# First layer of a hybrid decoder trunk: norm sums by TensorE, first chunk scaled from PSUM, k and q finished bank by bank

## The chip, the cores and the metric

The kernel runs on one core of one Trainium2 chip. The metric is device time in microseconds (us) of one launch, lower is better. All inputs lie in HBM when it starts and the result is written back to HBM.

## The reference

Two layers, each a token-mixing sub-layer and a SwiGLU sub-layer, on 512 tokens of width 1024 in float32. The change touches only the beginning of the first layer: the modulation, the norm of x, the first part of the input projection (k and q of the DeltaNet mixer) and what waits for it.

```python
c_act = jax.nn.silu(c)
for layer in range(DEPTH):
    mod = jnp.einsum('bd,de->be', c_act, w_mod[layer]) + b_mod[layer]
    shift1, scale1, gate1, shift2, scale2, gate2 = [m[:, None, :] for m in jnp.split(mod, 6, axis=-1)]
    h = rms_norm(x, mix_norm_w[layer]) * (1.0 + scale1) + shift1
    proj = jnp.einsum('btd,de->bte', h, w_in[layer])
    dn_qkv, dn_z, dn_a, dn_b, gm_uv, sw_qkv = jnp.split(proj, IN_SPLITS, axis=-1)
    y_a = deltanet_mixer(dn_qkv, dn_z, dn_a, dn_b, ...)   # causal conv of 4 taps and silu on q, k, v first
    ...
    x = x + gate1 * jnp.einsum('bte,ed->btd', y, w_out[layer])
    ...
```

`rms_norm` is `x * rsqrt(mean(x*x) + 1e-6) * w`, with the mean over the 1024 features.

## The kernel before, in words

x lies transposed in SBUF: 8 chunks `xs[0..7]` of 128 features by 512 tokens. The products are made in a three-pass form: both operands are split into a rounded part `hi` and a rest `lo` (type fp32r), and `mm3` issues hi·hi, hi·lo and lo·hi, each 128 rows by 128 columns of weights against 512 tokens. Splitting a weight piece takes one ACT instruction (`hi`) and one DVE instruction (`lo`).

Weights stream in as pieces of 512 KB: SP issues one DMA per piece into a ring of `N_RAW = 4` raw buffers, and a buffer comes free when its piece has been used. Weight pieces are split into a ring of `N_RING = 3` hi/lo pairs; a pair comes free when the matmuls that read it are done. In the first layer the pieces come in threes: two of the modulation matrix (`("mod", 0, c)` and `("mod", 0, 8 + c)`), then `("t", 0, c)`, which holds row chunk c of the weights of all 8 tiles of k and q. A modulation piece is consumed by one DVE instruction, a multiply with the broadcast condition and a sum along the row, that leaves one column of shift or scale.

`first()` does the start of the first layer, in coroutines that a planner interleaves:

- `squares()` takes each chunk of x as it lands: ACT squares it, DVE adds it to a running sum `a`, and `warm` issues a 128x256 matmul on it whose result nobody reads.
- `scale()` calls `inv_rms`: four matmuls of `a` with a column of ones give the sum over the features (128 tokens each, one output column each), DVE computes the reciprocal root (`rsqrt`, 9 small instructions), four matmuls with the identity broadcast it over the partitions into a bank, and ACT copies it into the SBUF slot `rs`.
- `chunk(c)` waits for `rs` and for the two modulation columns of c; ACT makes the gain `gg`, DVE multiplies x by gain and `rs` (`xn`), ACT adds the shift and rounds (`h[c].hi`), DVE makes the rest (`h[c].lo`).
- The main part then takes all 8 PSUM banks, one per tile of k and q, and runs chunk after chunk over all of them: 8 `mm3`, 24 matmuls, a chunk. All banks are complete only after the last chunk.

Then `layer` starts a `conv_of` on each of the 8 banks: ACT copies the bank to SBUF, which frees it, ACT scales the copy by the last tap, DVE adds three taps, ACT applies silu. The next projection, `ab`, needs four free banks.

What sets the order: there is no fixed list. `Plan` builds the program by running the coroutines against its own estimate of every instruction's duration, always taking the ready one with the lowest priority number, and each engine then executes its instructions in the order in which they were emitted. A change of a few instructions can therefore move others. The instructions are all recorded by one helper, so the profile gives L235 as the line of everything, and groups are told apart by the tiles' names: `w` a work slot, `xs` a chunk of x, `raw` a landed weight piece, `hi`/`lo` its split, `mod` the modulation columns, `s` a small tile, `cst` the constants (ones and identity among them), `b` a PSUM bank. A float32 matmul shows as two records on PE, an fp32r one as one.

Two places in `loader` and `splitter` matter below. The constants are loaded behind x:

```python
for c in range(KC):
    Q.dma_start(out=xs[c], in_=xT[:, c, :])
Q.dma_start(out=cst[:, 0:C_TRIU], in_=consts[:, 0:C_TRIU])
```

and a piece is split when the ring has room:

```python
if not raws[0] or (len(arena.free) < loose if loose else hold[0] or used[0] >= N_RING):
    return None
```

Of the kernel before, what the change touches and what calls it, by code (L numbers as in the profile page):

```python
# [88 lines left out]
class Plan:  # L89
# [106 lines left out]
    def spawn(self, gen, prio, name):  # L196
        t = Task(gen, prio, name)
        self.tasks.append(t)
        return t
# [84 lines left out]
def _trunk(ctx, tc, xT, cb, consts, prm, gmp, wmod, wt, wn, wab, wo, wo2, wf1, wf2, out):  # L284
# [29 lines left out]
    def bank(n=1, spare=0):  # L314

        yield banks.need(n + spare)
        got = [banks.get() for _ in range(n)]
        return got[0] if n == 1 else got
# [22 lines left out]
    def hs(h):  # L341
        return slice(h * P, (h + 1) * P)
# [175 lines left out]
    def wcols(w, j, n=128, pitch=None):  # L518
        if isinstance(w[0], list):
            return wcols((w[0][j * n // T], w[1][j * n // T]), j % (T // n), n)  # L520
        a = j * (pitch or n)
        return w[0][:, a:a + n], w[1][:, a:a + n]

    def mod_done(l, es):
        return tuple(mod_ok[l, e] for e in es)
# [28 lines left out]
    def mm3(ps, w, x, first, last):  # L554

        PE.matmul(ps, w[0], x[0], start=first, stop=False)
        PE.matmul(ps, w[0], x[1], start=False, stop=False)
        PE.matmul(ps, w[1], x[0], start=False, stop=last)
# [36 lines left out]
    def inv_rms(a, b0, n, warm=None):  # L595

        yield a[:, b0 * P:(b0 + n) * P]
        ps = yield from bank()
        for b in range(n):
            PE.matmul(ps[:, b:b + 1], a[:, hs(b0 + b)], ones[:, 0:1], start=True, stop=True)  # L600
        if warm:
            warm(a, 3)
        v = small(n)
        V.tensor_scalar(v, ps[:, 0:n], 1.0 / D, EPS, op0=ALU.mult, op1=ALU.add)
        bankf(ps)
        r = rsqrt(v, n)
        yield r
        rb = yield from bank()
        for b in range(n):
            PE.matmul(rb[:, hs(b0 + b)], r[:, b:b + 1].to_broadcast([P, P]), ident, start=True, stop=True)  # L610
        yield rb
        return rb
# [707 lines left out]

    def first():

        a = slot()

        bw = yield from bank()

        def warm(t, n=1):

            for _ in range(n):
                PE.matmul(bw[:, 0:256], t[:, 0:P], t[:, 0:256], start=True, stop=True)  # L1330

        def squares():
            yield x_ok
            for c in range(KC):
                yield S, xs[c]
                sq = slot() if c else a
                S.activation(sq, xs[c], AF.Square)
                yield V, sq
                warm(sq)
                if c:  # L1340
                    V.tensor_tensor(a, a, sq, op=ALU.add)
                    free(sq)

        sq = spawn(squares(), 0, "squares")
        rs = slot()

        def scale():
            yield sq
            rb = yield from inv_rms(a, 0, NB, warm)
            free(a)  # L1350
            S.activation(rs, rb, AF.Copy)
            bankf(rb)
            yield rs
            warm(rs, 3)
            bankf(bw)

        sc = spawn(scale(), 0, "scale")
        h = [Pair() for _ in range(KC)]

        def chunk(c):  # L1360
            yield sc, mod_done(0, (c, 8 + c))
            yield S, mods[0][:, c:c + 1], mods[0][:, 8 + c:9 + c]
            gg = small(1)
            nw = prs[0][:, L_NW + c:L_NW + c + 1]
            S.activation(gg, mods[0][:, 8 + c:9 + c], AF.Identity, scale=nw, bias=nw)
            yield V, gg
            xn = slot()
            V.scalar_tensor_tensor(xn, xs[c], gg, rs, op0=ALU.mult, op1=ALU.mult)
            yield S, xn
            h[c].hi, h[c].lo = slot(F32R), slot(F32R)  # L1370
            S.activation(h[c].hi, xn, AF.Identity, bias=mods[0][:, c:c + 1])
            yield V, h[c].hi
            V.scalar_tensor_tensor(h[c].lo, xn, mods[0][:, c:c + 1], h[c].hi[:].bitcast(F32), op0=ALU.add, op1=ALU.subtract)
            free(xn)
            h[c].ok[0].done = h[c].ok[1].done = True

        ts = [spawn(chunk(c), 0, f"h{c}") for c in range(KC)]
        yield sc
        pss = yield from bank(8)
        for c in range(KC):  # L1380
            w = yield from take("t", 0, c)
            x = yield from operand(h[c], FULL)
            for j in range(8):
                mm3(pss[j], wcols(w, j), x, c == 0, c == KC - 1)
                yield
            drop(w)
        yield tuple(ts)
        free(rs)
        return h, pss

    def layer(l, h, kq):

# [35 lines left out]
        def conv_of(i, ps):  # L1428
            return spawn(conv(ps, i, cw, AF.Silu if i < n_silu else AF.Tanh), rank()["conv" if i < 8 else "convv"], f"conv{i}")
# [94 lines left out]
        ts = spawn(gmlp(l, vg), rank()["gm"], "gmlp")  # L1524

        if l == 0:
            kT = [conv_of(i, ps) for i, ps in enumerate(kq[:4])]
            qT = [conv_of(4 + i, ps) for i, ps in enumerate(kq[4:])]

        def qss_of(qT):  # L1530
            r = yield from sumsq_heads(qT)
# [275 lines left out]
```

## Time and profile before

| | us |
|---|---|
| median of 3 runs | 1484.37 (1483.23 to 1485.97) |
| profiled execution, its own time | 1484.25 |
| span of its instructions | 1482.5 |
| TensorE (PE) busy | 1460.3 |
| DVE busy | 886.4 |
| ACT busy | 593.5 |
| mean granted clock of TensorE | 0.996 |

The span runs from the first to the last instruction; 1.75 us of the execution's own time lie around it. Busy time of an engine is the time covered by its records. The granted clock is given as a share of the full 2.4 GHz; 0.50 is 1.2 GHz. The clock column has no entry ahead of 13.83 us and shows 1.00 there, so that for the first 14 us the pace of the matmul records has to be read instead.

### The profile page before, as it was taken

Reading aid. Unit: us, or ns where it says so; the run is one execution under the profiler, and the core shown is the slowest. Engines: PE = TensorE matmul, PEld = TensorE weight load, DVE = VectorE, ACT = ScalarE, POOL = GpSimd, SP = SyncE. Lnnn points to the kernel's source line nnn. Section 1 sums busy time; section 2 is a strip of 40 time slices with the busy share of each in tenths; the row PEclk is TensorE's granted clock in tenths of the full one; section 3 lists DMA queues with packets and bytes.
Section 4 is the critical chain, followed back from the end, with each engine's and each line's share of the span. In section 5 each row is a group of like instructions: output and inputs, shape, how many; then the busy total and the mean of one; then the engine's idle time right before and its main releaser. Section 6 shows DMA issues by size and latency. Waiting matters only on the chain.

```text
span 1482.5 us, 19988 instructions
## 1 busy us (share of the span) xinstructions
PE 1460.3 (99%) x7810; PEld 1235.4 (83%) x7810; DVE 886.4 (60%) x1836; ACT 593.5 (40%) x1047; POOL 40.7 (3%) x60
## 2 busy tenths in 40 slices
PE   7999999999999999999999999999999999999998
PEld 5777998887988888888897889987789888888887
DVE  7788888946865555555476687656476333333332
ACT  4484426575432212222345533647544222222221
POOL 0001000000000000000000300100000000000000
PEclk9999999999999999999999999999999999999999
DMA  8723453503176665665322232121151332223331
GB/s 297 261 72 118 110 163 117 161 20 121 56 227 199 190 194 192 191 197 185 104 91 82 64 102 70 36 94 36 31 164 44 99 99 95 92 98 100 99 103 53
DMA packets 70638, 179.04 MB, mean 121 GB/s; under 512 B 25104, under 2 KB 25744, under 8 KB 70544
## 3 DMA queue, kind: packets, MB, share of 16 engines
q1 hardware_dynamic: 70544, 177.77, 37.5%
q8 instruction: 61, 1.00, 0.3%
q14 instruction: 33, 0.27, 0.1%
HBM read 174.53 MB, written 3.21 MB: 120 GB/s over the span
## 4 chain that ended last, share of the span: by engine, by line
PE 97%; DVE 1%; ACT 1%; DMA 0%; issue 0%; SPq 0%; ACTq 0%; DVEq 0%
PE b L235 97%; DVE w L235 1%; ACT w L235 1%; DMA xs<-in_xT_dram 0%; DVE s L235 0%; DVE raw L235 0%; DVE xs L235 0%; SPq L235 0%; DVE lo L235 0%; DVE mod L235 0%; ACT hi L235 0%; ACTq L235 0%; DVEq L235 0%
## 5 line engine op out<-in xcount | busy, mean ns | idle before, releaser
L235 PE MATMUL b<-w,hi 128*128 128x512 f32 (+1 forms) x2748 | 844.5, 389 | 2.5 <-ACT w L235 1.6
L235 PEld LDWEIGHTS b<-w,hi 128*128 128x128 f32 x2748 | 509.6, 188 | 110.8 <-issue 6.7
L235 PE MATMUL b<-w,lo 128*128 128x512 f32 (+1 forms) x1374 | 531.2, 387 | 0.0
L235 ACT ACTIVATE hi<-raw 128x1024 fp32r<-128x1024 f32 (+2 forms) x215 | 222.6, 1037 | 600.2 <-PE b L235 414.8
L235 DVE TENSOR_TENSOR lo<-raw,hi 128x1024 fp32r<-128x1024 f32 (+2 forms) x215 | 258.9, 1206 | 258.9 <-ACT hi L235 258.1
L235 PEld LDWEIGHTS b<-w,lo 128*128 128x128 f32 x1374 | 258.4, 188 | 52.3
L235 PE MATMUL b<-w,w 128*128 128x128 f32 (+2 forms) x1808 | 214.9, 284 | 4.0 <-ACT w L235 2.6
L235 PE MATMUL b<-hi,w 128*128 128x512 f32 (+2 forms) x768 | 214.8, 367 | 2.9 <-ACT w L235 2.9
L235 PEld LDWEIGHTS b<-w,w 128*128 128x128 f32 (+1 forms) x1808 | 199.2, 182 | 20.6 <-ACT w L235 10.2
L235 ACT ACTIVATE w<-b 128x512 f32<-128x512 f32 (+1 forms) x221 | 118.1, 560 | 137.0 <-PE b L235 126.0
L235 PEld LDWEIGHTS b<-hi,w 128*128 128x128 f32 x768 | 146.9, 213 | 24.1 <-issue 6.0
L235 PE MATMUL b<-lo,w 128*128 128x512 f32 (+2 forms) x384 | 137.7, 359 | 0.0
L235 DVE CUSTOM_DVE_ANT_0 raw<-raw,cact,pr 128x1024 f32<-128x1024 f32 x96 | 122.4, 1279 | 0.7 <-DMA raw<-in_wmod_dram 0.7
L235 DVE TENSOR_TENSOR w<-w,b 128x512 f32<-128x512 f32 x68 | 46.8, 688 | 125.5 <-PE b L235 124.7
L235 ACT ACTIVATE w<-w 128x512 f32<-128x512 f32 (+3 forms) x188 | 94.0, 519 | 22.9 <-DVE w L235 22.4
L235 PEld LDWEIGHTS b<-lo,w 128*128 128x128 f32 x384 | 81.4, 212 | 7.7
L235 DVE TENSOR_TENSOR w<-w,w 128x512 fp32r<-128x512 f32 (+2 forms) x104 | 68.1, 662 | 26.7 <-ACT w L235 26.1
L235 DVE SCALAR_TENSOR_TENSOR xs<-b,mod,xs 128x512 f32<-128x512 f32 (+1 forms) x56 | 37.1, 672 | 55.5 <-PE b L235 55.3
L235 PE MATMUL b<-cst,w 128*128 128x128 f32 (+1 forms) x416 | 57.5, 270 | 0.0
L235 PEld LDWEIGHTS b<-cst,w 128*128 128x128 f32 x416 | 49.4, 145 | 7.5 <-issue 1.0
L235 DVE SCALAR_TENSOR_TENSOR w<-w,cw,w 128x509 f32<-128x509 f32 (+2 forms) x72 | 51.8, 753 | 0.9 <-ACT w L235 0.2
L235 ACT ACTIVATE w<-w,mod 128x256 fp32r<-128x256 f32 (+1 forms) x56 | 29.8, 539 | 48.2 <-DVE w L235 48.2
(85 smaller groups left out, 652.4 us busy)
## 6 DMA issues: line engine op xcount, KB each, us to landing
raw<-in_wf_dram SPq DMA_DIRECT2D x132, 512.0 KB, 3.8
raw<-in_wmod_dram SPq DMA_DIRECT2D x96, 512.0 KB, 3.3
raw<-in_wt_dram SPq DMA_DIRECT2D x36, 512.0 KB, 3.5
raw<-in_wn_dram SPq DMA_DIRECT2D x36, 512.0 KB, 3.3
raw<-in_wo_dram SPq DMA_DIRECT2D x16, 320.0 KB, 2.9
raw<-in_wo_dram SPq DMA_DIRECT2D x6, 512.0 KB, 3.5
raw<-in_wab_dram SPq DMA_DIRECT2D x4, 544.0 KB, 5.7
xs<-in_xT_dram SPq DMA_DIRECT2D x8, 256.0 KB, 5.7
```

What stands on the lines that cost most here:

```text
L235: r = f(*args, **kw)
```

## The change

All of it is in `first()`, with one loop in `layer` that takes the banks as they come.

1. The running sum on DVE (7 additions of 128x512) goes. Instead, for every chunk, the four matmuls with a column of ones run on that chunk's square, and the eight chunks accumulate in one bank: 32 such matmuls in place of 4. The `warm` matmul stays, ahead of them; three `warm` behind the sums become two.
2. The broadcast reciprocal root is written over the same bank. Chunk 0 is multiplied from that bank instead of from the copy `rs`; the others wait for `rs` as before.
3. Chunks 0 to 5 run as before. Chunks 6 and 7 are taken together: for each bank, three matmuls of chunk 6 and three of chunk 7, after which the bank is handed to its `conv_of` at once.

```diff
@@ first() @@
-        a = slot()
...
-        def squares():
+        rs = slot()
+        got = Flag()
+
+        def scale():
+
             yield x_ok
+            ps = yield from bank()
+            sqs = [slot() for _ in range(KC)]
             for c in range(KC):
                 yield S, xs[c]
-                sq = slot() if c else a
-                S.activation(sq, xs[c], AF.Square)
-                yield V, sq
-                warm(sq)
-                if c:
-                    V.tensor_tensor(a, a, sq, op=ALU.add)
-                    free(sq)
-
-        sq = spawn(squares(), 0, "squares")
-        rs = slot()
-
-        def scale():
-            yield sq
-            rb = yield from inv_rms(a, 0, NB, warm)
-            free(a)
-            S.activation(rs, rb, AF.Copy)
-            bankf(rb)
+                S.activation(sqs[c], xs[c], AF.Square)
+                yield sqs[c]
+                warm(sqs[c])
+                for b in range(NB):
+                    PE.matmul(ps[:, b:b + 1], sqs[c][:, hs(b)], ones[:, 0:1], start=(c == 0 and b == 0), stop=(c == KC - 1),
+                              skip_group_check=True)
+            warm(sqs[KC - 1], 2)
+            v = small(NB)
+            V.tensor_scalar(v, ps[:, 0:NB], 1.0 / D, EPS, op0=ALU.mult, op1=ALU.add)
+            r = rsqrt(v, NB)
+            yield r
+            for b in range(NB):
+                PE.matmul(ps[:, hs(b)], r[:, b:b + 1].to_broadcast([P, P]), ident, start=True, stop=True)
+            got.value = ps
+            got.done = True
+            free(*sqs)
+            yield ps
+            S.activation(rs, ps, AF.Copy)
             yield rs
             warm(rs, 3)
             bankf(bw)
...
         def chunk(c):
-            yield sc, mod_done(0, (c, 8 + c))
+            yield got, mod_done(0, (c, 8 + c))
...
-            yield V, gg
+            rb = rs
+            if not c:
+                rb = got.value
+            else:
+                yield sc
+            yield V, gg, rb
             xn = slot()
-            V.scalar_tensor_tensor(xn, xs[c], gg, rs, op0=ALU.mult, op1=ALU.mult)
+            V.scalar_tensor_tensor(xn, xs[c], gg, rb, op0=ALU.mult, op1=ALU.mult)
+            if not c:
+                yield sc
+                bankf(rb)
...
-        for c in range(KC):
+        for c in range(KC - 2):
             w = yield from take("t", 0, c)
             x = yield from operand(h[c], FULL)
             for j in range(8):
-                mm3(pss[j], wcols(w, j), x, c == 0, c == KC - 1)
+                mm3(pss[j], wcols(w, j), x, c == 0, False)
                 yield
             drop(w)
-        yield tuple(ts)
-        free(rs)
-        return h, pss
+
+        def finish(done):
+
+            ws, x = [], []
+            for c in (KC - 2, KC - 1):
+                ws.append((yield from take("t", 0, c)))
+            for c in (KC - 2, KC - 1):
+                x.append((yield from operand(h[c], FULL)))
+            for j in range(8):
+                for i in range(2):
+                    mm3(pss[j], wcols(ws[i], j), x[i], False, i == 1)
+                    yield
+                done(j, pss[j])
+            drop(*ws)
+            yield tuple(ts)
+            free(rs)
+
+        return h, finish
@@ layer() @@
         if l == 0:
-            kT = [conv_of(i, ps) for i, ps in enumerate(kq[:4])]
-            qT = [conv_of(4 + i, ps) for i, ps in enumerate(kq[4:])]
+            both = []
+            yield from kq(lambda j, ps: both.append(conv_of(j, ps)))
+            kT, qT = both[:4], both[4:]
```

How the emitted order moves, at three places. In the rows, a name's first number is the buffer and the last one counts the tiles.

**PE, from the first square to the first product.** Before (from the sixth `warm` on):

```order
L235 MATMUL b_1_120<-w_7_141 128x256
L235 MATMUL b_1_120<-w_8_145 128x256
L235 MATMUL b_1_120<-w_9_149 128x256
L235 MATMUL b_2_156<-cst,w_1_119 128x1 x4
L235 MATMUL b_1_120<-w_1_119 128x256 x3
L235 MATMUL b_3_182<-cst,s_166 128x128 x4
L235 MATMUL b_1_120<-w_2_121 128x256 x3
L235 MATMUL b_4_203<-w_11_214,hi_178 128x512
```

Now (the first two chunks, and from the last chunk on):

```order
L235 MATMUL b_1_119<-w_2_122 128x256
L235 MATMUL b_2_121<-cst,w_2_122 128x1 x4
L235 MATMUL b_1_119<-w_3_123 128x256
L235 MATMUL b_2_121<-cst,w_3_123 128x1 x4
...
L235 MATMUL b_1_119<-w_9_129 128x256
L235 MATMUL b_2_121<-cst,w_9_129 128x1 x4
L235 MATMUL b_1_119<-w_9_129 128x256 x2
L235 MATMUL b_2_121<-cst,s_183 128x128 x4
L235 MATMUL b_1_119<-w_1_120 128x256 x3
L235 MATMUL b_3_225<-w_11_219,hi_195 128x512
```

The one-column matmuls with the ones (`cst`) stood once, behind all squares; now four stand behind every chunk's `warm`, the first four as PE's second entry.

**DVE, from its first instruction to the rest of chunk 0.** Before (the 7 additions come first; the reciprocal root's inner rows left out):

```order
L235 TENSOR_TENSOR w_1_119<-w_1_119,w_9_149 128x512
L235 ISA raw_111,mod_90<-raw_111,cact,pr_88 128x1024
...
L235 TENSOR_SCALAR s_164<-b_2_156 128x4
...
L235 SCALAR_TENSOR_TENSOR s_166<-s_167,s_166 128x4
L235 TENSOR_TENSOR lo_179<-raw_115,hi_178 128x1024
L235 ISA raw_113,mod_90<-raw_113,cact,pr_88 128x1024
...
L235 ISA raw_117,mod_90<-raw_117,cact,pr_88 128x1024
...
L235 SCALAR_TENSOR_TENSOR w_10_201<-xs_78,s_199,w_2_121 128x512
L235 ISA raw_154,mod_90<-raw_154,cact,pr_88 128x1024
...
L235 SCALAR_TENSOR_TENSOR w_12_215<-w_10_201,mod_90,w_11_214 128x512
```

Now, with the same rows left out:

```order
L235 TENSOR_SCALAR s_181<-b_2_121 128x4
...
L235 SCALAR_TENSOR_TENSOR s_183<-s_184,s_183 128x4
L235 TENSOR_TENSOR lo_196<-raw_115,hi_195 128x1024
L235 ISA raw_111,mod_90<-raw_111,cact,pr_88 128x1024
...
L235 ISA raw_113,mod_90<-raw_113,cact,pr_88 128x1024
...
L235 SCALAR_TENSOR_TENSOR w_10_217<-xs_78,s_215,b_2_121 128x512
L235 ISA raw_117,mod_90<-raw_117,cact,pr_88 128x1024
...
L235 SCALAR_TENSOR_TENSOR w_12_220<-w_10_217,mod_90,w_11_219 128x512
```

The root is now the first thing in DVE's order, and the first modulation column (`raw_111`), which stood ahead of it, stands behind it.

**ACT, at the end of k and q**, around the split of the first piece of `ab` (128x1088) and the last chunk of h. Before:

```order
L235 ACTIVATE s_481<-mod_90,pr_88 128x1
L235 ACTIVATE w_32_491<-w_31_483,mod_90 128x512
L235 ACTIVATE hi_497<-raw_434 128x1088
L235 ACTIVATE hi_528<-raw_448 128x1088
L235 ACTIVATE hi_558<-raw_467 128x1024
L235 ACTIVATE w_35_570<-b_4_203 128x512
```

Now:

```order
L235 ACTIVATE s_500<-mod_90,pr_88 128x1
L235 ACTIVATE hi_536<-raw_454 128x1088
L235 ACTIVATE w_34_539<-w_31_505,mod_90 128x512
L235 ACTIVATE w_37_556<-b_3_225 128x512
```

The split of `ab` has moved ahead of the rounding of chunk 7 (`w_34_539`); on DVE the rest of that split stands ahead of the rest of chunk 7 in the same way.

## Rows read from the trace of the kernel before

**Rows 1.** The page: busy us of the engines, share of the span, instructions.

```profile
PE 1460.3 (99%) x7810; PEld 1235.4 (83%) x7810; DVE 886.4 (60%) x1836; ACT 593.5 (40%) x1047; POOL 40.7 (3%) x60
```

**Rows 2.** Windows: busy time by stage (columns named in its first row).

```profile
core 0: us, PE busy (x) PEld busy (x) DVE busy (x) ACT busy (x) POOL busy (x), PEclk, DMA share, GB/s
...
23.04:68.25 45.21, 45.21 (x191) 36.93 (x191) 36.08 (x57) 15.40 (x23) 0.00 (x0) 0.96 0.83 289
68.25:90.39 22.14, 19.25 (x110) 15.60 (x109) 17.38 (x24) 16.92 (x28) 1.27 (x1) 0.85 0.22 71
90.39:1478.80 1388.41, 1383.02 (x7468) 1173.65 (x7466) 818.41 (x1728) 549.86 (x982) 39.24 (x55) 1.00 0.36 113
```

**Rows 3.** Timeline of PE: start, us, engine, records xcount, [idle before <-releaser].

```profile
7.94 6.18 PE L235 MATMUL b<-w 128*128 128x256 f32 x14 [0.66 <-ACT w L235]
13.96 0.95 PE L235 MATMUL b<-cst,w 128*128 128x1 f32 x8
14.77 1.54 PE L235 MATMUL b<-w 128*128 128x256 f32 x6
...
23.04 0.50 PE L235 MATMUL b<-w,hi 128*128 128x512 f32 x1 [0.61 <-DVE w L235]
```

**Rows 4.** Timeline of SP's queue: the constants' issue.

```profile
5.67 0.63 SPq L235 DMA_DIRECT2D cst<-in_consts_dram  x1
```

**Rows 5.** DMA issues of 5 to 12 us: KB each, us to landing.

```profile
cst<-in_consts_dram SPq DMA_DIRECT2D x1, 128.0 KB, 6.0
```

**Rows 6.** Timeline of ACT: squares of chunks 2 to 7, first gain.

```profile
8.09 3.85 ACT L235 ACTIVATE w<-xs 128x512 f32<-128x512 f32 x6 [0.20 <-DMA xs<-in_xT_dram]
...
19.28 0.39 ACT L235 ACTIVATE s<-mod,pr 128x1 f32<-128x1 f32 x1 [0.54 <-DVE mod L235]
```

**Rows 7.** Timeline of DVE, root to rest of chunk 0.

```profile
14.94 0.16 DVE L235 TENSOR_SCALAR s<-b 128x4 f32<-128x4 f32 x1 [0.32 <-PE b L235]
...
16.81 1.23 DVE L235 TENSOR_TENSOR lo<-raw,hi 128x1024 fp32r<-128x1024 f32 x1
17.95 1.28 DVE L235 CUSTOM_DVE_ANT_0 raw<-raw,cact,pr 128x1024 f32<-128x1024 f32 x1
...
20.36 0.75 DVE L235 SCALAR_TENSOR_TENSOR w<-xs,s,w 128x512 f32<-128x512 f32 x1
...
22.23 0.75 DVE L235 SCALAR_TENSOR_TENSOR w<-w,mod,w 128x512 fp32r<-128x512 f32 x1
```

**Rows 8.** Weight loads by form, 6 to 13.6 us: xcount, us, mean ns.

```profile
L235 PEld LDWEIGHTS b<-w 128*128 128x128 f32 x16 | 4.8, 323 | 8.7 <-ACT w L235 7.8
```

**Rows 9.** The same, 15 to 16.2 us.

```profile
L235 PEld LDWEIGHTS b<-w 128*128 128x128 f32 x5 | 1.0, 190 | 0.1
```

**Rows 10.** Windows: the two stretches at half clock.

```profile
24.07:27.48 3.41, 3.41 (x10) 2.67 (x9) 3.41 (x7) 1.24 (x2) 0.00 (x0) 0.50 0.90 311
71.86:78.68 6.82, 6.28 (x27) 5.97 (x28) 6.79 (x11) 6.66 (x12) 0.00 (x0) 0.50 0.23 77
```

**Rows 11.** Timeline of PE: the first four entries of ab.

```profile
69.70 0.51 PE L235 MATMUL b<-hi,w 128*128 128x264 f32 x2 [1.45 <-ACT w L235]
...
70.94 0.51 PE L235 MATMUL b<-hi,w 128*128 128x264 f32 x2 [0.61 <-ACT w L235]
...
72.19 0.81 PE L235 MATMUL b<-hi,w 128*128 128x264 f32 x2 [0.61 <-ACT w L235]
...
73.43 0.81 PE L235 MATMUL b<-hi,w 128*128 128x264 f32 x2 [0.21 <-ACT w L235]
```

**Rows 12.** Timeline of ACT: rounding of chunk 7, split of ab.

```profile
56.70 0.72 ACT L235 ACTIVATE w<-w,mod 128x512 fp32r<-128x512 f32 x1 [1.68 <-DVE w L235]
57.33 1.10 ACT L235 ACTIVATE hi<-raw 128x1088 fp32r<-128x1088 f32 x1
```

**Rows 13.** Timeline of DVE: rest of chunk 7, rest of ab's split.

```profile
57.45 0.75 DVE L235 SCALAR_TENSOR_TENSOR w<-w,mod,w 128x512 fp32r<-128x512 f32 x1 [0.79 <-ACT w L235]
58.46 1.29 DVE L235 TENSOR_TENSOR lo<-raw,hi 128x1088 fp32r<-128x1088 f32 x1 [0.25 <-ACT hi L235]
```

## The prediction

> **What bounds the kernel now.** I read the busy times first. TensorE is covered by records for 1460.3 of 1482.5 us [rows 1], so the end moves only with two things: when PE starts its dense work, and how long it stands still or runs at half clock afterwards. The table by stage shows where that is. Behind 90.39 us PE is busy for 1383.02 of 1388.41 us at full clock [rows 2]; nothing in that stage is edited (the planner shuffles some work of the first layer's DeltaNet part, all under PE). What the change can move lies ahead of it: the 23.04 us until the first unbroken product, the 45.21 us in which k and q run without a gap, and the 22.14 us behind, where PE is busy for 19.25 us only [rows 2].
>
> In the first stretch the PE timeline is to be read for its pace. From 7.94 to 13.96 us fourteen records of the 256-column `warm` take 0.43 us each; from 14.77 us on, six take 1.54, 0.26 each [rows 3]. So PE runs at half clock up to about 13.9 us, behind 6 us of back-to-back wide matmuls. Between the two groups stand the sums: eight one-column records (four matmuls, two records each) from 13.96 to the next group's start at 14.77, 0.10 us each, at full clock [rows 3]. DVE takes the root up at 14.94 [rows 7], and the first unbroken product comes 8.10 us later, at 23.04 [rows 3].
>
> **The sums: the largest term.** Two things about the new order matter. First, the sums multiply by the column of ones, and the ones are the last thing that is loaded behind x: issued at 5.67 [rows 4], landed 6.0 us later [rows 5], at 11.67. Before, nothing asked for them until 13.96. Now the first sums stand as PE's second entry, and everything behind them on PE, seven `warm` and all other sums, queues behind that landing. The squares go on and end at 11.94 [rows 6], but PE cannot use them yet. Second, there are 32 such matmuls, 64 records, where there were eight records.
>
> The price of one record at half clock is in no row. It is bounded by 0.10 us (no slower than at full clock) and 0.20 us (twice). I take the value by what paces them: each needs its own load of 128x128 weights, and that same form of load takes 323 ns in the half-clock stretch [rows 8] and 190 ns at full clock [rows 9], 1.7 times. So 0.17 us. I expect the half clock to last, since the stream is a `warm` of 0.86 us and then 1.36 us of one-column records, chunk after chunk.
>
> The last sum then ends at 11.67 + 64 x 0.17 + 7 x 0.86 = 28.6 us, and the root starts at about 28.8, with the 0.2 us that lie between the sums and DVE today [rows 3, 7]. Today it starts at 14.94 [rows 7]: **+13.9 us**. Nothing covers it: the root is now DVE's first instruction, so the modulation columns, which free the raw buffers, wait behind it, and SP's queue, which has only four raw buffers, waits behind them.
>
> A rule speaks for a smaller price. The Trainium skill, page "TensorE: Matmul & The Clock Gate", section "LDWEIGHTS (loading the stationary operand)", gives a load as its columns divided by 1.2 GHz, 107 ns here, and names no dependence on the gate; that agrees with 0.10 us at full clock and not with 323 against 190 ns. By that rule the sum below would come to 1490.9 us; it is the first rival.
>
> **From the root to the first product.** Removed are DVE's seven additions; they hid beside x's arrival, and DVE would now only idle in that time, so I cost them at nothing. In DVE's new order come the root (14.94 to 16.81 today, 1.87), the rest of the first weight piece (1.14, to 17.95), two modulation columns (2.41, to 20.36), a gain on ACT with its handovers (0.39 [rows 6], say 0.5), the product with x (0.7), one more modulation column (1.2), the rest of chunk 0 (0.75) and the handover to PE (0.1) [rows 7]: 8.7 us against 8.10 today, **+0.6 us**. Taking chunk 0 from PSUM saves a copy of 0.6 us on ACT, but the copy ran beside those two modulation columns, and does again. One modulation column, done ahead of the root today, moved behind it and makes up for the rest.
>
> The first products then run at half clock for a while, as today, where 3.41 us at 0.50 [rows 10] cost 1.7. PE does less ahead of them now, so I take 2.2, between 1.0 and 3.4: **+0.5 us**. From there k and q go at the pace of today, (45.21 - 1.7) / 192 = 0.227 us a matmul [rows 2, 10], 5.44 a chunk. The loads needed 289 GB/s for that [rows 2]; the ring starts with four pieces landed, so I expect it to keep up.
>
> **The last two chunks.** PE may start them only when chunk 7 is ready, one chunk earlier than today. And on ACT the split of `ab`'s first piece now stands ahead of the rounding of chunk 7. That split waits for a place in the hi/lo ring, which comes free with chunk 5's last matmul: today it starts at 57.33, right when chunk 5 is through, but behind the rounding of chunk 7 at 56.70 [rows 12]. Now chunk 7 queues behind it: the split (1.10 [rows 12]), on DVE the rest of the split (1.29) and the rest of chunk 7 (0.75) [rows 13] and three handovers (0.3) come to 3.4 us after chunk 5; four matmuls, 0.9 us, can run meanwhile. **+2.5 us** of standing still.
>
> **The handover.** Today all eight banks end together and `ab` waits for ACT to empty four: gaps of 1.45, 0.61, 0.61 and 0.21 us [rows 11], and then 6.82 us at half clock [rows 10], which cost 3.4. With a bank finished every 6 x 0.227 = 1.36 us and 1.3 us of ACT per bank, the first four are empty long before `ab` starts. All of it goes: **-6.3 us**.
>
> **Sum.** 13.9 + 0.6 + 0.5 + 2.5 - 6.3 = +11.2 us on the profiled execution's 1484.25, which is 0.1 below the median shown: 1495.4 us.
>
> **Rivals.**
> - *One-column records are no slower at half clock.* 64 x 0.10 instead of 64 x 0.17: the root at 24.3, +6.7 in all, 1490.9 us. For it: the full-clock pace is set by the loads, which need not follow the clock. Against it: rows 8 and 9. Chance 0.12.
> - *The clock rises within the sums.* PE is never idle from 11.67 on, and today it rose 6 us after back-to-back work began [rows 3]. Then 6 us at half clock bring 3.1 chunks, the other 4.9 go at 0.43 + 0.80 us each; the root starts at 23.9, +6.3 in all, 1490.5 us. Against it: 60% of the stream are one-column records, and between 71.86 and 78.68 the clock stayed at 0.50 although PE was busy for 6.28 of 6.82 us [rows 10]. The Trainium skill (the same page, "Part 1: The HAM clock gate") says that sustained activity releases the gate; no row here shows whether such a stream counts. Chance 0.15.
> - *Faster: the sums keep up with x.* If PE took them as the squares arrive, the root would start at 11.94 + 0.86 + 0.2 = 13.0, 1.9 us early, and the total would be -1.9 + 0.6 + 0.5 + 2.5 - 6.3 = -4.6: 1479.6 us. It decides for faster where the root starts before 17.6; from 11.67 on, at full clock, that needs a record in (17.6 - 11.9 - 3.0) / 64 = 0.04 us. The rows say 0.10, and the ones land at 11.67. Chance 0.03.
> - *The handover doesn't pay*, because ACT or DVE is behind and `ab` still waits: +11.2 + 6.3, 1501.8 us. ACT was idle for most of the stretch before [rows 2], against it. Chance 0.06.
>
> **How the numbers follow.** The forecast has 0.60; 0.04 is left for what I don't see. 0.2%, 3 us, is about what a measurement of this kernel can tell from no change. Within the forecast, 0.20 us a record puts the root at 30.7 and the time at 1497.3; a clock fall in the stop before chunk 7 adds 1.7: 1499. Down, the two cheaper cases reach 1490.5, and both together, full clock from the first sum, 1487.4. The range from 1489 to 1499 leaves out that corner, the faster case and the handover that doesn't pay. Faster 0.03, same 0.04, slower 0.93.
>
> **What would show it.** Right: PE idle from about 7 to 11.7 us, released by the constants' DMA; one-column records at 0.15 to 0.20 us; DVE's first instruction at 27 to 31 us; the first unbroken product near 37.5; a stop of 2 to 4 us behind chunk 5; no gap and full clock at `ab`. Wrong: a root before 22 us, `warm` records at 0.22 among the sums, or gaps ahead of `ab` as before.

## The result, and the profile after

The changed kernel takes **1518.69 us** (median of 5 runs, 1515.92 to 1519.84) against 1484.37: ratio 1.0225, 95% interval 1.0211 to 1.0239. It is slower, as forecast, but by 34 us and not by 11, outside the range. The profiled execution took 1515.92 us, 31.7 more than the one of before; its page answers to [rows 1]; it was the fastest of the five, so about 2.8 us of the difference between the medians are not in the profile:

```profile
PE 1478.9 (98%) x7864; PEld 1251.9 (83%) x7864; DVE 882.9 (58%) x1829; ACT 592.7 (39%) x1046; POOL 40.7 (3%) x60
```

PE is busy for 18.6 us more: it has 54 more records, and it spends more time at half clock. The windows by stage of the changed kernel, cut where [rows 2] cut them (columns: stretch, length, busy time of PE, PEld, DVE, ACT and POOL, granted clock, DMA share, GB/s), place the loss:

```profile
12.36:40.73 28.37, 25.66 (x97) 22.48 (x97) 7.86 (x20) 2.95 (x5) 0.00 (x0) 1.00 0.26 93
40.73:91.19 50.46, 46.76 (x191) 37.57 (x192) 44.10 (x70) 24.66 (x37) 1.28 (x1) 0.93 0.76 267
91.19:108.05 16.86, 16.86 (x109) 12.94 (x108) 10.72 (x16) 11.15 (x17) 0.00 (x0) 1.00 0.30 95
108.05:1510.00 1401.95, 1387.96 (x7467) 1178.34 (x7466) 819.43 (x1725) 546.75 (x979) 39.20 (x55) 1.00 0.35 112
```

The reader should subtract row by row. The first unbroken product comes at 40.73 instead of 23.04: +17.7. k and q take 50.46 instead of 45.21: +5.2. `ab` takes 16.86 instead of 22.14, PE busy in all of it: -5.3. The rest takes 1401.95 instead of 1388.41: **+13.5**, in a stage in which no instruction was edited. Together 31.2. Of the 13.5, PE's idle time accounts for 8.6 (13.99 against 5.39).

The timeline of PE shows the first stage (start, duration, engine, records, in brackets the idle time before and who ended it):

```profile
6.17 1.22 PE L235 MATMUL b<-w 128*128 128x256 f32 x2 [6.17 <-ACT w L235]
12.28 1.87 PE L235 MATMUL b<-cst,w 128*128 128x1 f32 x8 [4.89 <-DMA cst<-in_consts_dram]
14.01 1.20 PE L235 MATMUL b<-w 128*128 128x256 f32 x2
15.00 1.71 PE L235 MATMUL b<-cst,w 128*128 128x1 f32 x8
16.57 1.20 PE L235 MATMUL b<-w 128*128 128x256 f32 x2
...
31.93 2.05 PE L235 MATMUL b<-w 128*128 128x256 f32 x4
34.11 1.98 PE L235 MATMUL b<-cst,s 128*128 128x128 f32 x8
36.77 1.56 PE L235 MATMUL b<-w 128*128 128x256 f32 x6 [0.69 <-ACT w L235]
...
40.73 0.50 PE L235 MATMUL b<-w,hi 128*128 128x512 f32 x1 [0.61 <-DVE w L235]
```

PE waits 4.89 us for the ones, then a chunk takes 2.56 us from one `warm` to the next: 0.86 for the two records of `warm` (0.43 each, as in the half-clock group of [rows 3]) and 1.71 for eight one-column records, 0.214 each. That is half clock: six `warm` records take 1.56 us at full clock (36.77). DVE and SP stand behind it; these are DVE's first row and SP's row for the fifth raw buffer:

```profile
32.10 0.16 DVE L235 TENSOR_SCALAR s<-b 128x4 f32<-128x4 f32 x1 [32.10 <-PE b L235]
```

```profile
9.97 25.58 SPq L235 DMA_DIRECT2D raw<-in_wmod_dram  x2
```

The root starts at 32.10, 17.2 us later than in [rows 7], and SP stands in front of its next piece from 9.97 to 35.55.

In the second stage PE stops at one place, ahead of chunk 7; PE's two rows, then ACT's rows ahead of it, then DVE's product of chunk 7 with x:

```profile
77.54 0.79 PE L235 MATMUL b<-w,hi 128*128 128x512 f32 x1 [2.89 <-ACT w L235]
78.91 0.80 PE L235 MATMUL b<-w,hi 128*128 128x512 f32 x1 [0.58 <-DVE w L235]
```

```profile
71.87 1.06 ACT L235 ACTIVATE hi<-raw 128x1024 fp32r<-128x1024 f32 x1 [1.55 <-DMA raw<-in_wt_dram]
72.84 0.37 ACT L235 ACTIVATE s<-mod,pr 128x1 f32<-128x1 f32 x1
75.76 1.11 ACT L235 ACTIVATE hi<-raw 128x1088 fp32r<-128x1088 f32 x1 [2.55 <-DMA raw<-in_wab_dram]
76.78 0.71 ACT L235 ACTIVATE w<-w,mod 128x512 fp32r<-128x512 f32 x1
```

```profile
74.11 0.75 DVE L235 SCALAR_TENSOR_TENSOR w<-xs,s,w 128x512 f32<-128x512 f32 x1
```

DVE is done with that product at 74.8. ACT has nothing else to do then, but next in its order is the split of `ab`, whose piece lands only at 75.76, so chunk 7 is rounded at 76.78. About 1.9 us of the stop are this queue on ACT (an estimate: chunk 6's product begins at 68.82 and ACT rounds it 0.78 us later; chunk 7 is rounded 2.67 us after its product began). The rest is that chunk 7's own chain is late.

And in the last stage PE stops where it did not stop before, between 143 and 156 us:

```profile
147.14 0.66 PE L235 MATMUL b<-cst,w 128*128 128x128 f32 x4 [3.66 <-DVE w L235]
150.70 2.08 PE L235 MATMUL b<-w,w 128*128 128x128 f32 x8 [1.94 <-DVE w L235]
155.23 3.71 PE L235 MATMUL b<-w,w 128*128 128x128 f32 x16 [1.60 <-DVE w L235]
```

The granted clock of the changed kernel is full from 35.85 to 76.81, as the pace of the records there also says (so the first products lose nothing, unlike [rows 10]). It falls at three groups of stops, ahead of chunk 7, between 143 and 156 us and at about 795 us; windows of the four stretches:

```profile
35.85:76.81 40.96, 35.98 (x155) 28.53 (x154) 38.45 (x64) 16.63 (x25) 0.00 (x0) 1.00 0.91 314
76.81:83.64 6.83, 5.52 (x12) 4.09 (x13) 3.46 (x4) 2.87 (x6) 1.28 (x1) 0.50 0.69 265
148.49:158.73 10.24, 6.70 (x30) 6.04 (x30) 10.12 (x26) 6.17 (x18) 0.00 (x0) 0.50 0.00 0
797.02:800.44 3.42, 3.42 (x18) 3.42 (x17) 3.42 (x10) 2.06 (x5) 0.00 (x0) 0.50 0.00 0
```

Behind the stop ahead of chunk 7, PE is busy for 5.52 us at half clock, which loses about 2.8. In the last stage it is 6.70 + 3.42 us, about 5.1 lost: with the 8.6 of idle time that makes the 13.5, within 0.2. The same instructions are in the program before; what differs is their order. Alike instructions of PE stand 30.7 us later than before at 388 us and 31.7 later at the end, in an order that is the same from there on: nearly all of the 13.5 is lost in the first layer's DeltaNet and attention part.

### The profile page after: what moved, and what is told of

It is laid out like the page before. It is cut to its first block, busy times and chain, and to the rows that moved or that the text cites. A ratio compares the mean times of both kernels' runs of the same rounds, so it can differ in the third digit from the quotient of the medians.

```text
span 1514.1 us, 20076 instructions
## 1 busy us (share of the span) xinstructions
PE 1478.9 (98%) x7864; PEld 1251.9 (83%) x7864; DVE 882.9 (58%) x1829; ACT 592.7 (39%) x1046; POOL 40.7 (3%) x60
## 4 chain that ended last, share of the span: by engine, by line
PE 94%; DVE 3%; DMA 1%; ACT 1%; issue 0%; SPq 0%; ACTq 0%; DVEq 0%
PE b L235 94%; DVE w L235 1%; DMA raw<-in_wt_dram 1%; DVE lo L235 1%; DVE raw L235 1%; DMA raw<-in_wab_dram 0%; DMA cst<-in_consts_dram 0%; ACT hi L235 0%; ACT w L235 0%; SPq L235 0%; DVE s L235 0%; DVE xs L235 0%; DVE mod L235 0%; ACTq L235 0%; DVEq L235 0%
## 5 line engine op out<-in xcount | busy, mean ns | idle before, releaser
L235 PE MATMUL b<-w,w 128*128 128x128 f32 (+2 forms) x1808 | 220.2, 287 | 9.1 <-DVE w L235 4.7
L235 PEld LDWEIGHTS b<-w,w 128*128 128x128 f32 (+1 forms) x1808 | 204.0, 185 | 26.3 <-ACT w L235 11.0
L235 PE MATMUL b<-hi,w 128*128 128x512 f32 (+2 forms) x768 | 211.3, 363 | 0.0
L235 PEld LDWEIGHTS b<-hi,w 128*128 128x128 f32 x768 | 145.5, 209 | 20.8 <-issue 6.9
L235 PE MATMUL b<-cst,w 128*128 128x128 f32 (+1 forms) x472 | 71.9, 282 | 8.6 <-DMA cst<-in_consts_dram 4.9
L235 PEld LDWEIGHTS b<-cst,w 128*128 128x128 f32 x472 | 63.9, 170 | 17.4 <-DMA cst<-in_consts_dram 5.6
L235 DVE TENSOR_TENSOR w<-w,w 128x512 fp32r<-128x512 f32 (+2 forms) x97 | 63.2, 659 | 18.6 <-ACT w L235 18.5
L235 DVE SCALAR_TENSOR_TENSOR w<-w,cw,w 128x511 f32<-128x511 f32 (+2 forms) x72 | 51.5, 746 | 6.5 <-ACT w L235 5.9
```

Source lines behind the costliest of these rows:

```text
L235: r = f(*args, **kw)
```

## The experiments

`PR0` below is the first layer's table of priorities; a lower number is taken first. "Before" is run beside each group on the same chip: 1483.07 us for the first four kernels, 1484.49 for the next four, 1483.56 for the last four.

### One half of the change at a time

The finish alone: the kernel before, with only the loop over chunks 6 and 7 bank by bank and the handover.

```diff
-        for c in range(KC):
+        for c in range(KC - 2):
...
+        def finish(done):
...
-        return h, pss
+        return h, finish
```

> The kernel before with the last two chunks run bank by bank and handed over at once, and nothing else of the change: the sums stay on DVE. Theory A (the 15 us that the change lost in the DeltaNet part of the first layer, 108 to 388 us, come from the early handover of the banks): the first unbroken product stays at 23 us, the gaps ahead of ab go (-6.3 us), the stop ahead of chunk 7 costs 1 to 4 us, and PE stops of 7 us with a fall of the clock appear in the DeltaNet part as in the changed kernel: about 1490 to 1495 us. Theory B (those stops need the new start of the layer as well): no such block of stops, 1479 to 1484 us.

Measured: 1500.4 us (1500.1 to 1502.95), ratio 1.0119 [1.0104, 1.0134], above the figures of both theories. The handover works: PE has no gap in front of `ab`. But behind it, from 138 to 257 us, PE's timeline has fourteen waits; the longest and two others of them:

```profile
141.65 4.57 PE L235 MATMUL b<-w 128*128 128x128 f32 x24 [3.40 <-DVE w L235]
...
219.98 1.13 PE L235 MATMUL b<-w,w 128*128 128x128 f32 x8 [1.42 <-DVE w L235]
...
229.60 0.63 PE L235 MATMUL b<-cst,w 128*128 128x128 f32 x4 [1.90 <-DVE w L235]
```

So the loss behind the handover does not need the late root. The other half alone, the sums on TensorE and chunk 0 from the bank, without the finish:

```diff
-        for c in range(KC - 2):
+        for c in range(KC):
...
-        return h, finish
+        return h, pss
```

> The change without its last part: the sums on TensorE and chunk 0 from PSUM stay, k and q run chunk after chunk over all banks and are handed over together. Both theories: the root starts at 32 us, the first unbroken product near 40.7 us, and the gaps ahead of ab (2.9 us and a stretch of half clock) are back. Theory A (the stops in the DeltaNet part come from the early handover): none there, so 1484.3 + 17.7 - 1.7 = about 1500 us. Theory B (they come with the new start): 12 to 15 us more, about 1513 us.

Measured: 1509.17 us (1506.59 to 1509.88), 1.0171 [1.0156, 1.0187]: between the two figures. Its PE issues what the changed kernel's issues as far as chunk 6, in the same order, yet by the pace of its records the clock stayed at half until 45.3 us and not 36, and behind `ab` it has three stops of 1.46, 1.49 and 2.40 us. The halves cost 17.3 and 26.1 us alone and 34 together, so they don't add, and neither theory was settled.

### Two of the terms

The ones written into SBUF by GpSimd in place of the loaded column:

```diff
+    one = keep.tile([P, 1], F32, name="one")
+    G.memset(one, 1.0)
...
-                    PE.matmul(ps[:, b:b + 1], sqs[c][:, hs(b)], ones[:, 0:1], ...
+                    PE.matmul(ps[:, b:b + 1], sqs[c][:, hs(b)], one, ...
```

> The changed kernel with the column of ones written into SBUF by GpSimd at the start instead of waiting for the constants' DMA; PE's order is the same. If the wait for the constants is a cost of its own, PE starts the sums at 7.4 instead of 12.3 us and the root starts 4.9 us earlier, at 27.2 us; the whole time falls by 4 to 5 us to about 1514 us. If the sums were held up by the squares or by something else all the same, the root stays at 32 us and the time does not move.

Measured: 1509.25 us (1506.69 to 1511.02), 1.0169 [1.0152, 1.0186], 9.4 less than the changed kernel, twice what was expected. The root starts at 27.78, 4.3 us earlier. PE issues its records in the changed kernel's order, but ACT does not: it now rounds chunk 7 ahead of the split of `ab`, and PE stops there for 1.16 and 0.29 us in place of 2.89 and 0.58, with no half clock behind. This is taken up again below.

The split of `ab` held back until chunk 7 is ready:

```diff
+                if key[0] == "ab" and key[1] == 0 and not h7.done:
+                    return None
...
+            h7.done = c == KC - 1
```

> The changed kernel in which the split of the first piece of ab has to wait for the last chunk of h, so that chunk 7 no longer queues behind it; the planner then emits another order for the DeltaNet part. Theory A1 (the stop of 2.9 + 0.6 us ahead of chunk 7 and the half clock behind it come from the queue on ACT): that stop shrinks to below 1.5 us and the clock stays up, 5 to 6 us less there. Theory A2 (chunk 7 is late by itself, because its loads are): the stop stays above 2 us. In the DeltaNet part: if the stops at 143 to 155 us belong to the emitted order alone, they go, and the whole time falls by 12 to 20 us, to about 1500 us; if DVE is simply too slow there whatever the order, PE stops there for about 7 us as before, and the time falls by 5 us at most.

Measured: 1521.45 us (1520.72 to 1522.6), 1.0258 [1.0243, 1.0273]. The stop ahead of chunk 7 is still there, 3.0 us in place of 3.5, although on ACT chunk 7 now stands ahead of `ab` (PE's rows, then ACT's):

```profile
76.95 0.49 PE L235 MATMUL b<-w,hi 128*128 128x512 f32 x1 [2.33 <-ACT w L235]
78.15 0.79 PE L235 MATMUL b<-w,hi 128*128 128x512 f32 x1 [0.71 <-DVE w L235]
```

```profile
73.16 1.06 ACT L235 ACTIVATE hi<-raw 128x1024 fp32r<-128x1024 f32 x1 [2.45 <-DMA raw<-in_wt_dram]
74.13 0.37 ACT L235 ACTIVATE s<-mod,pr 128x1 f32<-128x1 f32 x1
76.18 0.72 ACT L235 ACTIVATE w<-w,mod 128x512 fp32r<-128x512 f32 x1 [1.68 <-DVE w L235]
77.01 1.11 ACT L235 ACTIVATE hi<-raw 128x1088 fp32r<-128x1088 f32 x1
```

Here chunk 7 is late by itself: its piece lands 1.3 us later than in the changed kernel (ACT splits it at 73.16 and not 71.87), and DVE takes the rest of that piece before it scales x. That ate up most of what the shorter queue on ACT gave back. So this run doesn't acquit the split of `ab`: in the changed kernel it is about 1.9 us of the stop, by the rows shown there, and in both kernels with the memset (above, and at the end), where ACT rounds chunk 7 first, the stop is 1.5 us or none. The stops at 143 to 156 us are gone in this kernel, others stand at 159 and from 238 to 279 us. The first of them:

```profile
162.86 4.57 PE L235 MATMUL b<-w 128*128 128x128 f32 x24 [3.40 <-DVE w L235]
```

It is the stop that the finish alone has at 141.65, and the other two rows shown there come again too, 1.42 us at 241.19 and 1.90 at 250.81, each 21.2 us later. From the last sums on, the two kernels issue PE's records in the same order. The same order loses the same time behind two different starts.

### The order alone

This led to the theory that the priority table fits one timing of the start, and that almost any shift makes the planner give the DeltaNet part a worse order. It can be tested with no instruction changed. The entries below are such that the order they give has no late step in that part as far as the kernel's own planner sees.

In the changed kernel, two entries:

```diff
-            convv=0.2, E=2.2, B=1.8, blocks=0.2, kss=0.2, ...
+            convv=0.2, E=1.5, B=1.8, blocks=0.2, kss=1.8, ...
```

> The changed kernel with two entries of the first layer's priority table altered (E 2.2 to 1.5, kss 0.2 to 1.8); no instruction is added or taken away, only the order in which the DeltaNet part is emitted changes, so everything up to the end of k and q should read as in the changed kernel. Theory A (about 15 us are lost behind the handover because the priority table, which fits the old times, now gives an order in which PE waits for ACT and DVE): the stops of 3.66, 1.94 and 1.60 us and the half clock around 148 us go, 1502 to 1507 us. Rival B (the loss is work of ACT and DVE that used to be done beside k and q and has to be done later, in whatever order): 1515 to 1520 us, with the stops at other places.

Measured: **1504.11 us** (1503.45 to 1505.93), 1.0139 [1.0125, 1.0153]: 14.6 us back between the medians, 10.0 between the two profiled executions. Its timeline of PE has two waits between `ab` and 360 us that are longer than 0.3 us:

```profile
116.41 1.05 PE L235 MATMUL b<-w,cst 128*32 128x512 f32 x2 [0.96 <-ACT w L235]
...
350.06 3.54 PE L235 MATMUL b<-w,w 128*64 128x128 f32 x32 [0.69 <-ACT w L235]
```

The second stands in the kernel before too, at 329.58. From 156 us of the kernel before on, PE's records come in the same order in both, and they stand 20.8 us later there and 20.5 later at 362: behind the late start, that order loses nothing. The rival, work that has to be done later in any order, falls. One part of the expectation failed: up to 95 us the order is that of the changed kernel, but the stop ahead of chunk 7 is 4.49 and 0.88 us here, with the piece of `ab` landing at 77.02 and not 75.76. Between these two profiles the stop differs by 1.9 us with the order unchanged.

In the kernel with the finish alone, two other entries:

```diff
-... swin=5, ... scales=1.8, ...
+... swin=1.5, ... scales=0, ...
```

> The kernel of the first experiment (before with only the finish bank by bank) with two entries of the first layer's priority table altered (swin 5 to 1.5, scales 1.8 to 0). Theory A: the handover's 6.3 us are kept and the stops behind it go, 1476 to 1480 us, under the kernel before. Rival B: 1496 to 1502 us as without the two entries.

Measured: **1481.07 us** (1480.2 to 1484.73, 11 runs), 0.9984 [0.9975, 0.9992]. It is 19.3 us under the same program with the old entries and the only kernel here whose interval lies under the one before, though by less than 0.2%. The gain is smaller than expected: `ab` takes 16.88 us here, 5.3 less than before, but 2 us of that are lost again by 355 us, 1.5 of them in two waits at 334 us:

```profile
68.68:85.56 16.88, 16.88 (x109) 12.95 (x108) 12.60 (x19) 10.60 (x18) 0.00 (x0) 1.00 0.30 95
```

```profile
335.15 0.49 PE L235 MATMUL b<-w,hi 128*128 128x512 f32 x1 [1.17 <-ACT w L235]
335.94 0.50 PE L235 MATMUL b<-w,hi 128*128 128x512 f32 x1 [0.30 <-DVE w L235]
```

The kernel before, with only the planner's price of a one-column matmul changed:

```diff
-            full = 0.0004167 * (256 if passes == 4 and n <= 64 and m == 128 else n) * passes * ...
+            full = 0.0004167 * (128 if passes == 4 and n == 1 and m == 128 else 256 if ... else n) * passes * ...
```

> The kernel before with the planner's own price of a one-column float32 matmul halved, which is near what the trace shows for it; no instruction of the program differs, only the order from the first layer's DeltaNet part on. Theory A (the order of before is one at which the table fits; nearly any other costs time): 1488 to 1497 us, with new stops of PE between 120 and 330 us. Rival B (orders of this part are alike, it is the handover or the late root that costs): 1482 to 1486 us.

Measured: 1496.27 us (1495.23 to 1498.25), 1.0086 [1.0072, 1.0099]. A truer price in the planner costs 11.8 us, because it shifts the planner's clock by a little and with it the order.

And the kernel before with the two entries that served the finish, its only edit:

```diff
-... swin=5, ... scales=1.8, ...
+... swin=1.5, ... scales=0, ...
```

> The kernel before with the same two entries as in the kernel of the run on the finish with two entries (swin 1.5, scales 0), no other edit. Theory A (the numbers fit one timing of the handover alone): slower than before, 1494 to 1506 us, with stops of several us between 110 and 130 us. Rival B (the two numbers are merely better in general, and the finish has no part in it): 1478 to 1484 us.

Measured: 1498.22 us (1496.97 to 1500.59), 1.01 [1.0085, 1.0116], with these stops among others in PE's timeline:

```profile
125.88 0.66 PE L235 MATMUL b<-cst,w 128*128 128x128 f32 x4 [2.51 <-DVE w L235]
130.77 2.08 PE L235 MATMUL b<-w,w 128*128 128x128 f32 x8 [3.23 <-DVE w L235]
135.30 1.16 PE L235 MATMUL b<-w,w 128*128 128x128 f32 x8 [1.60 <-DVE w L235]
```

The same two numbers take 19.3 us off one program and put 13.7 on the other. They are not better numbers: which order the table gives depends on the start.

### The terms again, on an undisturbed order

The changed kernel without the `warm` ahead of each chunk's sums:

```diff
                 yield sqs[c]
-                warm(sqs[c])
                 for b in range(NB):
...
-... vv=5,
+... vv=0,
```

> The changed kernel without the warm matmul ahead of each chunk's sums, and with one priority entry (vv 5 to 0) that gives an order without the stops behind the handover. Theory C (a stream of one-column matmuls stays at half clock whatever stands between, 0.214 us a record): the root starts 7 x 0.86 = 6.0 us earlier, near 26 us instead of 32.1, the first products may lose 2 to 3 us at half clock, 1499 to 1503 us, 2 to 5 under the changed kernel with two priority entries (1504.1). Rival D (the warm matmuls keep the clock from rising, or the bare stream lets it rise): records at 0.107 us, root near 20 us, 1493 to 1497 us. Rival E (the warm matmuls bring the clock up for the first products, and without them it stays down through several chunks): 1504 to 1508 us.

Measured: 1498.73 us (1498.07 to 1499.48), 1.0101 [1.0087, 1.0114]; 5.4 under the kernel with two entries. The timeline of PE:

```profile
11.56 13.78 PE L235 MATMUL b<-cst,w 128*128 128x1 f32 x64 [11.56 <-DMA cst<-in_consts_dram]
25.21 2.05 PE L235 MATMUL b<-w 128*128 128x256 f32 x4
27.38 2.01 PE L235 MATMUL b<-cst,s 128*128 128x128 f32 x8
30.08 1.56 PE L235 MATMUL b<-w 128*128 128x256 f32 x6 [0.69 <-ACT w L235]
```

64 records in 13.78 us, 0.215 each, and the four wide records behind them still take 0.51 each: PE was never idle and the clock stayed at half. At 30.08 it is full, and the first products lose nothing. So the `warm` among the sums were 6 us for nothing. The time is just under the figures of theory C.

The memset once more, with the two entries that served the changed kernel:

```diff
+    G.memset(one, 1.0)
...
-... E=2.2, ... kss=0.2, ...
+... E=1.5, ... kss=1.8, ...
```

> The changed kernel with the column of ones written by GpSimd instead of loaded, and the two priority entries E 1.5 and kss 1.8. Against 1504.1 us (the same entries, ones loaded) it gives the price of the wait for the constants alone. If the 9.4 us that the same edit took off without the entries were half order: 4.5 us less, 1498 to 1501 us. If all 9.4 were the wait: 1494 to 1496 us. If the wait is covered by the arrival of x: 1503 to 1505 us.

Measured: 1494.74 us (1493.67 to 1496.65), 1.0076 [1.006, 1.0091], 9.4 under the kernel with two entries. So the 9.4 of the first try were not half the order of the DeltaNet part. The windows from the root to `ab` and from `ab` on show where they lie, of the kernel with two entries and of this one:

```profile
31.31:93.02 61.71, 52.85 (x211) 41.71 (x212) 52.12 (x89) 26.32 (x40) 1.28 (x1) 0.94 0.70 238
93.02:1500.00 1406.98, 1400.90 (x7574) 1187.65 (x7573) 823.99 (x1740) 556.34 (x995) 42.42 (x55) 1.00 0.36 113
```

```profile
27.56:82.51 54.95, 50.79 (x210) 40.82 (x211) 51.39 (x87) 26.32 (x40) 1.37 (x1) 0.97 0.77 267
82.51:1489.00 1406.49, 1399.95 (x7575) 1186.24 (x7573) 824.83 (x1742) 556.36 (x995) 42.43 (x55) 1.00 0.36 113
```

The root is 3.8 us earlier, and the stretch up to `ab` is 6.8 us shorter: here PE does not stop ahead of chunk 7, where the kernel with two entries stops for 4.49 and 0.88 us and then runs at half clock. PE's order is the same in both, but ACT's and DVE's are not, and at chunk 7 ACT's rows are:

```profile
70.84 0.72 ACT L235 ACTIVATE w<-w,mod 128x512 fp32r<-128x512 f32 x1 [1.68 <-DVE w L235]
71.59 1.11 ACT L235 ACTIVATE hi<-raw 128x1088 fp32r<-128x1088 f32 x1
```

Chunk 7 is rounded first and `ab` is split behind it. The time is that of the second case, but the wait for the ones is only about 4 us of it; the rest hangs on the stop ahead of chunk 7, which is gone with the order moved at that place. PE's first products also wait longer here and run at half clock for 3.4 us, which gives chunk 7's chain more time; no run takes the two apart.

The third part of the change, chunk 0 from the bank, on the kernel with the finish and its two entries:

```diff
             free(a)
+            got.value = rb
+            got.done = True
             S.activation(rs, rb, AF.Copy)
-            bankf(rb)
...
-            yield sc, mod_done(0, (c, 8 + c))
+            yield got, mod_done(0, (c, 8 + c))
...
+            rb = rs
+            if not c:
+                rb = got.value
+            else:
+                yield sc
```

> The kernel of the run on the finish with two priority entries (1481.07 us) plus the third part of the change, chunk 0 scaled from the bank instead of from the copy; the sums stay as before. If the copy was hidden beside two modulation columns: no change within 0.6 us, 1480.4 to 1481.7. If the copy stood on the path of the first product: up to 0.6 us less. If DVE is slower from PSUM or the bank held longer delays the first products: 1482 to 1483.

Measured: 1482.8 us (1480.92 to 1485.51, 11 runs), 0.9995 [0.9986, 1.0003]: no gain. From the root to the first `lo` product it is 8.42 us here and 8.44 without; the copy was hidden. That is the time of the third case but not by its mechanism: the first products are not late, PE waits 0.56 and 0.70 us ahead of chunk 7 in place of 0.28. The intervals of the two ratios touch, so a loss is not shown either.

The same program with another pair of entries:

```diff
-... swin=1.5, ... scan=0.2, ... scales=0, ... split=0.1, ...
+... swin=5, ... scan=0.6, ... scales=1.8, ... split=0, ...
```

> The same program as in the run on the finish with chunk 0 from PSUM, with two other priority entries (split 0.1 to 0, scan 0.2 to 0.6) instead of swin and scales: another order of the DeltaNet part for which the plan has no stop there. Theory A (the order alone decides what the handover is worth): within 2 us of it, 1478 to 1482. Rival: the first pair of entries was a lucky hit, and this one falls back to 1490 or more.

Measured: 1482.96 us (1480.95 to 1484.61, 11 runs), 0.9995 [0.9986, 1.0004]. That is 1 us above the figures named, and far from the rival's 1490. A second order without long stops gives the same time: the first pair was no lucky hit.

## Why the prediction was wrong in size

**The step that failed** is the sentence that nothing is edited behind 90.39 us and that the planner's shuffling is "all under PE". It was costed at nothing and measured 13.5 us of the 31.2 between the two profiles. The cover named, PE's own work, was not there: in the new order PE waited for DVE between 143 and 156 us and then ran at half clock. Five kernels show that the order does this and not the edits as such: two entries of the table give 14.6 us back in the changed kernel and 19.3 in the finish alone, and cost 13.7 in the kernel before, a changed price costs 11.8 there, and a second pair of entries gives the same low time as the first. The same order also loses, or saves, the same time behind another start. Why each of the bad orders is bad was not followed to its end; the runs show that the order is the cause, not which single step in it.

**The one-column record was mis-sized.** I took 0.17 us from the ratio of two load durations, 323 and 190 ns [rows 8, 9]. It measured 0.214, above the upper bound of 0.20. The durations were right (loads at half clock take 334 ns in the changed kernel), but they overlap; the pace is the distance from one record's start to the next, and that about doubled, from 0.101 over the eight records of [rows 3] at full clock to 0.214 at half. That is 2.8 us. Another 0.6 is that the ones were there at 12.28 and not at 11.67 (in two later runs at about 11.5). The root came at 32.10 and not at 28.8, +3.3 us. By the Trainium skill ("TensorE: Matmul & The Clock Gate", "LDWEIGHTS (loading the stationary operand)") a load of 128 columns takes 107 ns, with no word of the gate; that comes near 0.101 at full clock and not 0.214, and the measurement decides.

**Right:** the wait for the ones (PE idle from 7.4 to 12.28 us, ended by the constants' DMA), the half clock through all sums, the root as DVE's first instruction, and 8.6 us from the root to the first product where 8.7 were forecast. The rival in which the clock rises within the sums fell; it had also counted a full-clock `warm` as 0.43 us, where [rows 3] has two records of 0.26. The Trainium skill (the same page, "Part 1: The HAM clock gate") has sustained activity release the gate; PE busy without a pause for 13.78 us of one-column records did not release it here.

**Right in mechanism, too small:** the stop ahead of chunk 7 came, 2.89 and 0.58 us where 2.5 were forecast, and chunk 7 did queue on ACT behind the split of `ab`, for about 1.9 us. But ACT waited there for `ab`'s piece to land (75.76), not only for a place in the ring, and chunk 7's own chain was late as well. The stop brought 6.83 us at half clock, 5.52 of them busy, about 2.8 lost, which the prediction had priced at 1.7 and only for its upper end. In return the first products ran at full clock, 1.7 better than before where 0.5 worse was forecast. That PE, with the first products at full clock, runs into chunk 7's chain sooner is likely but not shown. The stretch as a whole cost 5.2 us and not 3.0.

**The handover** paid 5.3 us where 6.3 were forecast, and 5.3 again in the kernel with the finish and two entries. The gaps of 2.9 us went as forecast; the half clock was priced at half of 6.82 us, 3.4, but PE was busy for only 6.28 of them [rows 10], and its busy time in `ab` fell by 2.4 (19.25 to 16.86). There was no gap and no half clock at `ab`, as forecast.

## What to carry to other kernels

When an order is made by a planner with tuned priorities, an edit that shifts the start also changes the order far behind it: cost that as a term of its own, with the size that a harmless shift has (here 12 to 19 us), and judge an edit only after its order has been tuned again. Take the pace of pipelined instructions from the distance between their starts, not from their durations. And ask what a stop does beyond its own length: here a stop of 3.5 us was followed by half clock that cost about another 2.8. When a kernel waits on a queue, look at what stands ahead in that engine's order and what that one waits for: here a split that waited for its load held up a chunk that was ready.

## What was not expected of the hardware

A stream of 64 one-column float32 matmuls, 13.78 us without a pause, left TensorE at 1.2 GHz: 0.215 us a record from first to last, and 0.51 for the wide records behind it, against 0.26 at full clock. The same stream with a wide matmul of 0.86 us in front of every eight records but the first, 19.7 us long, did no better.

When the clock rises is not settled by the instructions alone. The changed kernel and the one with the sums alone give PE the same work in the same order as far as chunk 6. The changed kernel issues six `warm` in 1.56 us at 36.77; the other runs its first products at half clock, as these rows of its PE show, two records in 1.05 us and soon after in 0.62:

```profile
44.32 1.05 PE L235 MATMUL b<-w,hi 128*128 128x512 f32 x2
...
46.18 0.62 PE L235 MATMUL b<-w,hi 128*128 128x512 f32 x2
```
